# Storing the gate/up operands of later passes in pairs, with their order made to fit and one sum moved between passes

## The chip, the cores and the metric

The kernel runs on one core of a Trainium2 chip. The metric is the time of one execution in microseconds (us), measured on the device; less is better. Each engine has its own instruction stream: TensorE (PE in the profile, PEld for its weight loads), VectorE (DVE), ScalarE (ACT), GpSimd (POOL) and SyncE (SP), which here issues transfers. The granted clock is TensorE's clock as a share of its full speed, the DMA share the mean busy share of the 16 DMA engines, SBUF the memory on the chip that the engines work in.

## The reference

```python
def reference(x, w_gate, w_up, w_down):      # x: 8 x 1024 x 1024, float32; hidden 1024, intermediate 4096
    gate = x @ w_gate
    up = x @ w_up
    gate = 0.5 * gate * (1 + np.tanh(np.sqrt(2 / np.pi) * (gate + 0.044715 * gate ** 3)))
    h = gate * up
    return (h @ w_down).astype(np.float32)
```

## The kernel before

The kernel works on 1024 tokens at a time, in 8 passes. Each pass has a gate/up stage and a down stage. The block products are not the plain ones: passes 0 to 2 use a scheme with 7 products for each 2 x 2 block ("pairs" of block columns, 16 a pass), later passes a finer one whose left operands are 24 signed sums of weight blocks for each of 8 column groups. Those 24 operands are not made when they are needed. They are made once, 12 in pass 1 and 12 in pass 2, in the idle time of VectorE (sums) and ScalarE (plain signed copies), and stored in a DRAM tensor `wop`, from which passes 3 to 7 load two at a time, in rows of 4 KB.

```python
A_PARTS = ([8, 11, 12, 13, 16, 18, 22, 24, 25], [9, 10, 14, 15, 17, 19, 20, 21, 23])
wop = nc.dram_tensor("w_ops", (NQ, NCH, P, 2, 1024), FP16, kind="Internal").ap()
...
    def make_entry(p, q, e):
        n, sign = A_ENTRIES[e]
        v = place[q, n] = places[turn[0] % len(places)]      # 12 slots in SBUF, used in turn
        turn[0] += 1
        if n < 8:                                            # a raw block: a copy on ScalarE
            nc.scalar.activation(four(v), a_node(p, q, n), COPY, scale=float(sign))
        else:                                                # a sum of two nodes: VectorE
            _, op, a, b = A_SUMS[n - 8]
            combine(four(v), op, a_node(p, q, a), a_node(p, q, b))
        nc.sync.dma_start(out=wop[q, e // 2, :, e % 2], in_=v)   # half of each 4 KB row
...
    # gate_up_one, inside the loop over the 16 pairs i = 2 q + e of passes 1 and 2:
            for j, n in enumerate(entries_of(p - FAST + 2)):
                if j // 6 == e:
                    at(2 * (j % 6) + 2, make_entry, p, q, n)     # after products 2, 4, ... 12 of the pair
```

A pair is 14 products of 4 matmuls each. The products are summed in PSUM banks, the buffers that TensorE writes; the next product that takes a bank must wait until VectorE or ScalarE has read what it needs there (an eviction). The order of products and what follows each of them matters below (w is 0 for gate and 1 for up; cut and set closer than in the kernel):

```python
SEQ = [
    ("P1", 0), ("P1", 1), ("P5", 0), ("P6", 0), ("P6", 1), ("P5", 1), ("P7", 0),
    ("P7", 1), ("P2", 0), ("P4", 0), ("P4", 1), ("P2", 1), ("P3", 0), ("P3", 1),
]
AFTER1 = {   # after product k: evictions by ScalarE (copy, snap, gelu), sums by VectorE (add, h)
    1: ["copy 0"], 2: ["copy 1"], 4: ["snap s2 0"], 5: ["snap s2 1"], 7: ["snap s3 0"],
    8: ["snap s3 1", "add s3 0"], 9: ["gelu11", "gelu s3", "add s3 1"],
    10: ["gelu21", "prod s3"], 11: ["h21"], 12: ["h11"], 13: ["add s2 0"], 14: ["add s2 1"],
}
CHAIN = {"P1": "a", "P6": "a", "P7": "a", "P4": "a", "P5": "b", "P3": "b", "P2": "c"}   # PSUM bank
```

## Time and profile before

| | before |
|---|---|
| time, median of 3 runs | 2256.19 us (2256.08 to 2257.9) |
| profiled span, granted clock | 2254.4 us, 1.0 |
| TensorE busy | 2246.1 us |
| gate/up of pass 1 and of pass 2, each | 193.39 us |
| DMA share there | 0.91 and 1.00 |
| stores of operands | 192 of 256 KB, in rows of 2 KB |

The profile is read from the engine that sets the end. Its waits tell what holds it up, and the chain of waits shows which stretch of time belongs to whom. A busy share of another engine, and the DMA share too, says nothing of the end as long as TensorE waits for none of it. The prediction shows the lines.

### The profile page before, as it was taken

The page shows a single profiled execution, that of the slowest core. Times are in us where ns is not written, and L with a number is a line of the kernel's source. Part 1 is how long each engine was busy: PE and PEld are TensorE (multiplying, and loading weights), DVE is VectorE, ACT ScalarE, POOL GpSimd, SP SyncE. Part 2 cuts the span into 40 slices and gives each one's busy share as a digit, 9 for nine tenths or more (in the row PEclk, how much of TensorE's full clock was granted, in tenths as well). Part 3 has the DMA queues.
Part 4 walks back from the last instruction along what each step waited for, and adds up shares of the span by engine and source line. Part 5 has one row for each costly group of instructions (what it writes and reads, how often), then busy time and mean ns, then how long its engine had stood idle before and what let it go on. Part 6 is the DMA issues. An engine that isn't in the chain of part 4 may idle for free.

```text
span 2254.4 us, 42805 instructions
## 1 busy us (share of the span) xinstructions
PE 2246.1 (100%) x16634; PEld 1625.6 (72%) x16634; DVE 1561.7 (69%) x2190; ACT 956.1 (42%) x1866; POOL 679.3 (30%) x825
## 2 busy tenths in 40 slices
PE   9999999999999999999999999999999999999999
PEld 4444444444444445888888888888888888888888
DVE  6576458883588755777776677666786667866674
ACT  4444135651355622666125550356404653055520
POOL 1332013330133200555014550255403543044520
PEclk9999999999999999999999999999999999999999
DMA  9898969989999999999998999989999889988876
GB/s 241 163 207 218 284 184 241 263 264 283 255 227 249 282 309 349 328 342 370 302 339 274 317 304 318 322 270 324 311 324 316 285 308 326 311 311 277 289 285 225
DMA packets 308093, 642.46 MB, mean 285 GB/s; under 512 B 79088, under 2 KB 185328, under 8 KB 287344
## 3 DMA queue, kind: packets, MB, share of 16 engines
q1 hardware_dynamic: 253104, 566.57, 73.2%
q0 software_dynamic: 54784, 73.14, 19.3%
q8 instruction: 130, 2.13, 0.4%
q14 instruction: 75, 0.61, 0.1%
HBM read 574.36 MB, written 138.41 MB: 316 GB/s over the span
## 4 chain that ended last, share of the span: by engine, by line
PE 87%; DMA 2%; SPq 0%; DVE 0%; issue 0%; DVEq 0%
PE ps L848 40%; PE ps L1099 20%; PE ps L626 17%; PE ps L991 10%; DMA wd_quads<-x_sums 1%; SPq L255 0%; DMA ring<-wd_ops 0%; DVE x_sums L452 0%; DVE h_a L923 0%; DVE tmp L1168 0%; DVE x_sums L278 0%; SPq L487 0%; DVEq L278 0%; SPq L535 0%
## 5 line engine op out<-in xcount | busy, mean ns | idle before, releaser
L848 PEld LDWEIGHTS <-ring 128*128 128x128 f16 x8320 | 814.1, 98 | 94.4
L825 POOL TENSOR_TENSOR h_a<-tmp 128x256 f16<-128x256 f32 x640 | 469.3, 753 | 839.3 <-ACT tmp L813 831.9
L848 PE MATMUL ps<-x_sums,ring 128*128 128x256 f16 x5760 | 655.8, 273 | 0.0
L810 DVE TENSOR_TENSOR tmp<-tmp,ps 128x512 f32<-128x512 f32 x640 | 414.5, 683 | 148.1 <-PE ps L848 99.7
L626 PEld LDWEIGHTS <-ring 128*128 128x128 f16 x2632 | 257.5, 98 | 310.4
L795 ACT COPY tmp<-ps 128x512 f32<-128x512 f32 x520 | 304.1, 585 | 237.5 <-PE ps L848 162.8
L626 PE MATMUL ps<-x_sums,ring 128*128 128x512 f16 x1504 | 339.8, 379 | 0.0
L813 ACT ACTIVATE tmp<-tmp 128x256 f32<-128x256 f32 x640 | 264.1, 418 | 172.8 <-DVE tmp L808 79.4
L848 PE MATMUL ps<-x_b,ring 128*128 128x256 f16 x2560 | 305.6, 273 | 0.0
L808 DVE TENSOR_TENSOR tmp<-ps,tmp 128x512 f32<-128x512 f32 x240 | 165.4, 689 | 145.2 <-ACT tmp L795 101.0
L626 PE MATMUL ps<-x_b,ring 128*128 128x512 f16 x1128 | 259.1, 379 | 0.0
L652 POOL TENSOR_TENSOR h_a<-tmp 128x512 f16<-128x512 f32 x94 | 144.5, 1537 | 374.8 <-ACT tmp L650 271.9
L1099 PEld LDWEIGHTS <-h_a 128*128 128x128 f16 x2240 | 219.2, 98 | 25.4
L991 PE MATMUL ps<-ring,h_a 128*128 128x512 f16 x1024 | 222.3, 379 | 0.4 <-DMA ring<-wd_ops 0.4
L1099 PE MATMUL ps<-ring,h_a 128*128 128x256 f16 x1920 | 216.1, 273 | 0.0
L991 PEld LDWEIGHTS <-h_a 128*128 128x128 f16 x1152 | 112.7, 98 | 136.6 <-DMA ring<-wd_ops 0.9
L645 DVE TENSOR_TENSOR tmp<-ps,tmp 128x512 f32<-128x512 f32 x188 | 127.2, 683 | 112.6 <-ACT tmp L637 111.1
L1156 ACT ACTIVATE tmp<-ps 128x512 f32<-128x512 f32 x60 | 35.3, 597 | 362.6 <-PE ps L1099 274.6
L1168 DVE SCALAR_TENSOR_TENSOR tmp<-ps,tmp 128x512 f32<-128x512 f32 x120 | 81.1, 690 | 97.5 <-PE ps L1099 66.6
L351 DVE TENSOR_TENSOR ring<-ring 128x1024 f16<-128x1024 f16 x188 | 138.7, 751 | 11.1 <-DMA ring<-in_w_up_dram 6.9
L637 ACT COPY tmp<-ps 128x512 f32<-128x512 f32 x188 | 109.9, 586 | 77.8 <-PE ps L626 77.8
L1099 PE MATMUL ps<-ring,x_sums 128*128 128x256 f16 x1120 | 126.3, 273 | 0.0
(102 smaller groups left out, 1532.0 us busy)
## 6 DMA issues: line engine op xcount, KB each, us to landing
ring<-w_ops SPq DMA_DIRECT2D x480, 512.0 KB, 5.0
ring<-wd_quads SPq DMA_DIRECT2D x110, 1024.0 KB, 7.0
ring<-wd_ops SPq DMA_DIRECT2D x35, 1024.0 KB, 8.2
out_dram<-tmp SPq DMA_DIRECT2D x128, 256.0 KB, 6.6
w_ops<-h_s SPq DMA_DIRECT2D x128, 256.0 KB, 6.7
ring<-in_w_gate_dram POOLq DMA_DIRECT2D x23, 1024.0 KB, 10.5
ring<-in_w_up_dram POOLq DMA_DIRECT2D x23, 1024.0 KB, 17.8
wd_quads<-x_sums SPq DMA_DIRECT2D x131, 128.0 KB, 6.4
```

What stands on the lines that cost most here:

```text
L351: nc.vector.tensor_tensor(o, a, b, op)
L626: nc.tensor.matmul(ps(b, w), lhs[:, k], rhs[:, k, :], start=(first and k == 0), stop=(k == KH - 1), skip_group_check=True,)
L645: nc.vector.tensor_tensor(o, ps("b", w), o, ADD)
L652: nc.gpsimd.tensor_tensor(hq[TO[n]][:, i, :], tmp[:, t[n, 1]], tmp[:, t[n, 0]], MUL)
L795: nc.scalar.copy(tmp[:, t[o[1]]], ps_all[:, bank[o[2]]])
L808: nc.vector.tensor_tensor(d, b, a, SUB)
L810: nc.vector.tensor_tensor(d, a, b, ADD if o[4] == "add" else SUB)
L813: nc.scalar.activation(d, d, GELU, scale=GSC)
L825: nc.gpsimd.tensor_tensor(h, tmp[:, t[o[1]], MQ : 2 * MQ], g, MUL)
L848: nc.tensor.matmul(ps_all[:, bank[c], w * MQ : (w + 1) * MQ], lhs[:, w, k], rhs[:, k], start=(first and w == 0 and k == 0), stop=(k == KH ...
L991: nc.tensor.matmul(ps_all[:, bank[b, g]], lhs[:, j, g * P : (g + 1) * P], dc[:, n, :], start=(first and j == 0), stop=(j == NP - 1), skip_ ...
L1099: nc.tensor.matmul(ps_all[:, bank[c], m * MQ : (m + 1) * MQ], lhs[:, j, m * P : (m + 1) * P], rhs[:, j, :], start=(first and j == 0 and m ...
```

## The change

The intent is to make transfers cheaper in the two stages that make operands. Two operands that share a 4 KB row are made one after the other, lie side by side in SBUF and are stored by one transfer. To get such neighbours the order of the 24 operands is written out by hand, and sum 21 goes from pass 2 to pass 1 while a plain copy goes the other way (in full: copies 2 and 3 go to pass 2 and copy 7 comes to pass 1). Below, "the order" means the written-out order with this exchange, as opposed to the wider stores.

```diff
--- before.py
+++ after.py
@@ -60,7 +60,10 @@
     (23, 22, 4, False),
 ]
 
-A_PARTS = ([8, 11, 12, 13, 16, 18, 22, 24, 25], [9, 10, 14, 15, 17, 19, 20, 21, 23])
+A_PARTS = (
+    [16, 8, 11, 12, 22, 21, 25, 24, 13, 4, 18, 7],
+    [9, 3, 10, 23, 2, 15, 17, 20, 14, 6, 19, 1],
+)
 
 AFTER = {
     1: [('snap', 's8', 1)],
@@ -356,6 +359,7 @@
         xc[:, j * 1024 : (j + 1) * 1024] for j in range(8, 12)
     ]
     turn = [0]
+    made_last = [None]
 
     def four(v):
         return v.rearrange("p (w k n) -> p w k n", w=2, k=KH)
@@ -375,18 +379,20 @@
         else:
             _, op, a, b = A_SUMS[n - 8]
             combine(four(v), op, a_node(p, q, a), a_node(p, q, b))
-        nc.sync.dma_start(out=wop[q, e // 2, :, e % 2], in_=v)
+
+        if turn[0] % 2 == 0 and e % 2 and made_last[0] == (q, e - 1):
+            k = (turn[0] - 2) % len(places)
+            v = hf["s3"][:, k * 1024 : (k + 2) * 1024] if k < 8 else xc[:, k * 1024 : (k + 2) * 1024]
+            nc.sync.dma_start(
+                out=wop[q, e // 2], in_=v.rearrange("p (e n) -> p e n", e=2)
+            )
+        elif (e ^ 1) not in entries_of(0 if p < FAST - 1 else 1):
+            nc.sync.dma_start(out=wop[q, e // 2, :, e % 2], in_=v)
+        made_last[0] = (q, e)
 
     def entries_of(part):
-        sums = [n for n, _, _, _ in A_SUMS if n in A_PARTS[part]]
-        plain = [n for n, _ in A_ENTRIES if n < 8][3 * part : 3 * part + 3]
-        nodes = []
-        for j, n in enumerate(sums):
-            nodes.append(n)
-            if j % 3 == 1:
-                nodes.append(plain[j // 3])
         ids = [n for n, _ in A_ENTRIES]
-        return [ids.index(n) for n in nodes]
+        return [ids.index(n) for n in A_PARTS[part]]
 
 
 
```

Two operands of each pass still have their partner in the other pass (11 and 23, 12 and 10); those are stored alone.

## The prediction

> **What bounds the kernel now.** I read first the busy times of the page, then the waits of TensorE alone, then the chain that ended last in order of time, then busy time by stage and by pair of column blocks, and last the queue's waits.
>
> The page's first part, a total for each engine:
>
> ```profile
> span 2254.4 us, 42805 instructions
> PE 2246.1 (100%) x16634; PEld 1625.6 (72%) x16634; DVE 1561.7 (69%) x2190; ACT 956.1 (42%) x1866; POOL 679.3 (30%) x825
> ```
>
> TensorE is busy for all but 2254.4 - 2246.1 = 8.3 us. A busy matmul row can hide a slow one, so the total is not yet proof. The waits of TensorE alone (engine and line, what it waited for: us in total, times, longest) name everything it ever waited for:
>
> ```profile
> PE ps L1219 <- DVE h_s L1222: 1.6, 1, 1.6
> PE ps L1198 <- DVE x_b L305: 1.1, 2, 0.6
> PE ps L1198 <- ACT ring L331: 0.6, 1, 0.6
> PE ps L991 <- DMA ring<-wd_ops: 0.4, 1, 0.4
> PE ps L303 <- DVE h_a L297: 0.2, 1, 0.2
> ```
>
> All are of pass 0: its warm-up and first pair, and one load in its down projection. None is on a line that pass 1 or 2 reaches with a wait. The chain in order of time (start us, us, what) shows the rest as one unbroken TensorE stretch from 279.69 to 2250.10 us:
>
> ```profile
> 279.69 27.80 PE ps L991 x128
> 307.50 193.39 PE ps L626 x896
> 500.88 96.69 PE ps L991 x448
> 597.57 193.39 PE ps L626 x896
> 790.96 96.69 PE ps L991 x448
> 887.65 181.68 PE ps L848 x1664
> ```
>
> The two rows of 193.39 us are gate/up of passes 1 and 2, the only stages that the change edits. They have the same length to 10 ns, and 193.39 / 896 = 0.2158 us for a 512-column matmul; the stage after takes 181.68 / 1664 = 0.1092 us for one of 256 columns. That is a steady rate, not a rate with holes in it.
>
> **What the Trainium skill says.** "TensorE: Matmul & The Clock Gate", section "Back-to-back issue gap", gives N / 2.4 + 2.5 ns at full clock: 215.8 ns for 512 columns and 109.2 for 256. The trace agrees to a tenth of a nanosecond, so these stages are at the matmul rate itself. (The same section's other figure, 131 ns sustained at N=512, is not seen here.) "Perfetto Trace Analysis", section "DMA Optimizations", says that going from 2 KB to 4 KB transfers is the primary remedy "when HBM utilization is high but DMA-bound". The first half holds in passes 1 and 2 (DMA share 0.91 and 1.00 in the table below), the second doesn't: TensorE waits for no transfer there. "SBUF — State Buffer", section "Who interferes with whom", says that a VectorE instruction with two SBUF inputs contends with a GpSimd one that reads SBUF. The trace fits that: the same half-width sum takes 0.41 us at its usual and 1.74 us at 407.90 us, beside a GpSimd product. So one more sum on VectorE may cost more than its usual 0.68 us.
>
> **The change part by part.** Busy time by stage (stretch, length, then PE, PEld, DVE, ACT, POOL busy with counts, granted clock, DMA share, GB/s), gate/up of pass 1 and of pass 2:
>
> ```profile
> 307.50:500.88 193.38, 193.38 (x897) 87.66 (x896) 155.87 (x241) 115.46 (x190) 62.79 (x44) 1.00 0.91 237
> 597.57:790.96 193.39, 193.39 (x898) 87.65 (x896) 154.67 (x241) 115.25 (x190) 61.74 (x46) 1.00 1.00 256
> ```
>
> *Stores.* Each of 8 column groups makes 24 operands, 12 in each pass. Before, each is stored alone: 8 x 24 = 192 transfers of 256 KB in rows of 2 KB. After, five of the six double slots a pass hold both members of a storage pair, made one after the other; two operands a group have their partner in the other pass (23 and 11, 10 and 12). So 8 x 2 x (5 + 2) = 112 transfers; a comparison of the two builds confirms 1249 rows of the transfer queue against 1169, and the same instructions in the same order on TensorE. Bytes are unchanged. In the trace's packets the median 2 KB packet of these stages takes 84 to 86 ns and the 4 KB packet of later stages 159 ns, so two for one saves some 11 ns. 80 transfers x 128 rows x 11 ns / 16 engines = 7 us of DMA time out of about 370, plus 80 x 0.32 us = 26 us of issuing on a queue that mostly sleeps. On the path: 0, for nothing waits for these stores before pass 3, where the first comes due long after.
>
> *One sum moved.* Node 21 goes from pass 2 to pass 1, a plain signed copy the other way. 8 sums x some 0.75 us (0.68 alone, 0.88 to 0.95 in the groups that meet GpSimd) = 6 us: VectorE in pass 1 from 155.9 to about 162, in pass 2 from 154.7 to about 149. 8 copies x 1.054 us = 8.4 us: ScalarE from 115.5 to about 107 and from 115.3 to about 124. Both stay far below 193.4. On the path: 0 as long as the order within a pair holds, which is the real question.
>
> *The order within a pair.* A pair of blocks takes 193.39 / 16 = 12.09 us of TensorE. Two neighbouring pairs of pass 1:
>
> ```profile
> 404.20:416.28 12.08, 12.08 (x57) 5.49 (x56) 12.08 (x20) 7.18 (x12) 4.44 (x4) 1.00 0.92 180
> 416.28:428.37 12.09, 12.09 (x57) 5.49 (x56) 8.95 (x17) 7.94 (x13) 4.60 (x3) 1.00 1.12 316
> ```
>
> VectorE is full in the even pair and lags; in the odd one it idles 3.1 us and catches up. In pass 1 the even pair now carries six sums in place of five. In pass 2 it carries four in place of five, so pass 2 gets easier here. What can bite TensorE is the first bank that a late VectorE gives back: product h21 of one pair releases the bank that the third product of the next pair takes. I set each h21's end against that product's start (pair start plus two products of 0.863 us). The margin in pass 1's even pairs is 1.4 us at the least (the pair at 404.20) and 1.9 to 3.4 in the others. A sum of 0.68 us ahead of it leaves 0.7 at the least, so still no wait.
>
> ScalarE in pass 2 has a similar spot: a 1.05 us copy now falls after the fourth product of even pairs, between two evictions of 0.585 us. The second eviction has 1.10 us in hand today. It then ends at about 4.08 + 1.05 + 0.59 = 5.7 us of the pair against a bank needed at 7 x 0.863 = 6.04: some 0.35 us left. The sum over all parts is 0.0 us.
>
> **The rivals.**
> *A new wait of TensorE on VectorE or ScalarE.* For it: margins of 0.7 and 0.35 us are small, and a sum that meets GpSimd can take a microsecond longer. Against it: only one pair of pass 1 comes near, and pass 2's copy has no other copy in front of it. If four pairs lost 0.3 us each, it would make 1.2 us: about 2257.4. If all 16 even pairs lost half a microsecond, 8 us: 2264, still the same verdict.
> *Transfers as the hidden bound, so that wider rows pay.* For it: a DMA share of 0.9 to 1.0, and the queue's own waits (126.8 us on VectorE in front of these stores, shown below). Against it: those waits end with the sum that the store needs, not with a transfer, and TensorE's list has no transfer after 280 us. The whole of what it could give is the 0.4 us there, in a stage that isn't changed: 2255.8.
>
> ```profile
> SPq L378 <- DVE h_s L278: 126.8, 73, 3.9
> SPq L378 <- DMA w_ops<-h_s: 5.6, 8, 1.1
> ```
>
> *A late slot.* A pair's first operand waits for its second before its store starts, so its slot comes free later, by about 1.7 us. There are 12 slots and 12 operands in two pairs of blocks (24.2 us), and stores land in 3.5 to 7 us; worth 0.
>
> **Range and chances.** Nothing is removed from TensorE's 2246.1 us and nothing that it waited for is touched, so the time stays at the median of before, 2256.2 us. Downward only run-to-run spread counts (2256.08 to 2257.9 before) and at most 0.4 us; upward the same spread and a few small new waits. I take 2255.2 to 2258.6. Two per cent is 45 us. Faster by that would need work taken off TensorE, which doesn't happen; slower would need 2.8 us lost in each of the 16 even pairs, more than the largest delay I can construct. Chances 0.005 faster, 0.985 the same, 0.01 slower.
>
> **What would show it.** Right: the chain again has two TensorE rows of 193.39 us; the list of TensorE's waits has the same five rows; 80 stores of 512 KB and 32 of 256 KB; VectorE and ScalarE near 162 and 107 us in pass 1, 149 and 124 in pass 2; a slightly lower DMA share there. Wrong: a new row in TensorE's waits for an eviction or a sum, most likely in the even pairs of pass 1, with rows over 193.39 us; or a shorter row, which would mean that the matmul rate itself depends on the stores and my reading of the bound is false.

## The result, and the profile after

The changed kernel took 2256.88 us (median of 6 runs, 2254.42 to 2257.2), the kernel before 2256.44 us in 6 runs beside it (2256.08 to 2257.9). The ratio is 0.9999 with a 95% interval of 0.9986 to 1.0012: the same. A ratio here is the mean time of one kernel's fast runs over that of the other's of the same rounds, so it is not quite the ratio of the medians quoted.

The changed file has six more lines, so line numbers in its profile are larger: L632 is before's L626 (matmuls of gate/up), L997 is L991 (down), L651 is L645 (the adds), L281 is L278 (the sums), L378 is L374 (the plain copies). The page's totals, and the waits of TensorE alone:

```profile
span 2255.0 us, 42663 instructions
PE 2245.1 (100%) x16634; PEld 1625.1 (72%) x16634; DVE 1558.5 (69%) x2190; ACT 954.9 (42%) x1866; POOL 676.3 (30%) x825
```

```profile
PE ps L1225 <- DVE h_s L1228: 1.6, 1, 1.6
PE ps L306 <- DVE h_a L300: 1.5, 2, 1.3
PE ps L997 <- DMA ring<-wd_ops: 1.2, 1, 1.2
PE ps L1204 <- DVE x_b L308: 1.1, 2, 0.6
PE ps L1204 <- ACT ring L334: 0.6, 1, 0.6
```

They are the same five, all in pass 0. Two of them have other sizes (1.5 for 0.2 us, 1.2 for 0.4); in the experiments below, whose pass 0 has the same instructions up to that point, the transfer's wait is anything from 0 to 2.5 us and that for h_a from 0.3 to 1.8 us in total, so this is spread. The chain that ended last, in order of time:

```profile
308.55 193.39 PE ps L632 x896
501.94 96.69 PE ps L997 x448
598.63 193.39 PE ps L632 x896
```

The two rows that the change could touch have 193.39 us, to the digit what they had. Busy time by stage (pass 1, pass 2; columns as in the prediction):

```profile
308.55:501.94 193.39, 193.39 (x897) 87.67 (x896) 158.90 (x248) 108.15 (x183) 64.66 (x44) 1.00 0.90 236
598.63:792.01 193.38, 193.38 (x897) 87.69 (x896) 148.21 (x233) 122.16 (x199) 58.04 (x46) 1.00 1.00 255
```

Everything moved except the time. VectorE went from 155.87 to 158.90 us in pass 1 and from 154.67 to 148.21 in pass 2; ScalarE from 115.46 to 108.15 and from 115.25 to 122.16. The DMA share hardly moved. The stores themselves did get cheaper, as the queues' lines in pass 1 show (packets, MB, share of 16 engines; q1 carries what SyncE issues, q0 what GpSimd issues, mostly the casting loads, which turn float32 weights into float16), first before, then after:

```profile
q1 hardware_dynamic: 18421, 32.75, 48.0%
q0 software_dynamic: 12762, 12.85, 42.3%
```

```profile
q1 hardware_dynamic: 12729, 32.67, 45.9%
q0 software_dynamic: 12768, 12.86, 44.0%
```

The same bytes in nearly a third fewer packets took 2.1 points of 193.4 us less, 4.1 us; the loads on the other queue, with the same bytes and packets, took 1.7 points more, 3.3 us.

### The profile page after: what moved, and what is told of

It reads as the page before. It is cut to its first block, busy times and chain, and to the rows that moved or that the text cites. A ratio compares the mean times of both kernels' runs of the same rounds, so it can differ in the third digit from the quotient of the medians.

```text
span 2255.0 us, 42663 instructions
## 1 busy us (share of the span) xinstructions
PE 2245.1 (100%) x16634; PEld 1625.1 (72%) x16634; DVE 1558.5 (69%) x2190; ACT 954.9 (42%) x1866; POOL 676.3 (30%) x825
## 4 chain that ended last, share of the span: by engine, by line
PE 99%; DMA 1%; DVE 0%; SPq 0%; ACT 0%; issue 0%; DVEq 0%
PE ps L854 40%; PE ps L632 25%; PE ps L1105 20%; PE ps L997 13%; PE ps L1204 1%; DMA ring<-wd_ops 0%; DMA x_sums<-in_w_gate_dram 0%; DVE x_b L308 0%; SPq L297 0%; ACT ring L334 0%; PE ps L306 0%; DVE tmp L1174 0%; DVEq L308 0%
## 5 line engine op out<-in xcount | busy, mean ns | idle before, releaser
L632 PEld LDWEIGHTS <-ring 128*128 128x128 f16 x2632 | 257.6, 98 | 310.3
L632 PE MATMUL ps<-x_sums,ring 128*128 128x512 f16 x1504 | 339.8, 379 | 0.0
L632 PE MATMUL ps<-x_b,ring 128*128 128x512 f16 x1128 | 259.1, 379 | 0.0
L997 PE MATMUL ps<-ring,h_a 128*128 128x512 f16 x1024 | 222.3, 379 | 1.2 <-DMA ring<-wd_ops 1.2
L997 PEld LDWEIGHTS <-h_a 128*128 128x128 f16 x1152 | 112.6, 98 | 137.4 <-DMA ring<-wd_ops 1.7
L651 DVE TENSOR_TENSOR tmp<-ps,tmp 128x512 f32<-128x512 f32 x188 | 127.8, 686 | 114.4 <-ACT tmp L643 112.6
```

The lines of the kernel that those rows point to most:

```text
L632: nc.tensor.matmul(ps(b, w), lhs[:, k], rhs[:, k, :], start=(first and k == 0), stop=(k == KH - 1), skip_group_check=True,)
L651: nc.vector.tensor_tensor(o, ps("b", w), o, ADD)
L997: nc.tensor.matmul(ps_all[:, bank[b, g]], lhs[:, j, g * P : (g + 1) * P], dc[:, n, :], start=(first and j == 0), stop=(j == NP - 1), skip_ ...
```

## The experiments

Twelve kernels ran. Where a gate/up row is quoted for a kernel whose chain breaks it into pieces, it is the time from its first matmul to the first of the next stage, read from the matmuls' starts in the trace. Margins below are read from the matmuls' starts too. The rows of the chain begin 0.16 to 0.17 us later than the first matmul of the stage (307.50 for 307.33 us), because they begin where the modelled end of the matmul before lies; the prediction and the expectations took pairs' starts from the chain, so their margins are that much too wide.

### 1. The order without the wider stores

```diff
-        if turn[0] % 2 == 0 and e % 2 and made_last[0] == (q, e - 1):
-            ...one transfer for both...
-        elif (e ^ 1) not in entries_of(0 if p < FAST - 1 else 1):
-            nc.sync.dma_start(out=wop[q, e // 2, :, e % 2], in_=v)
+        nc.sync.dma_start(out=wop[q, e // 2, :, e % 2], in_=v)
```

> The changed kernel with its new order of operands, but each operand stored alone in rows of 2 KB (192 stores of 256 KB). My theory (TensorE sets the end; neither part of the change is on its path): two gate/up rows of 193.39 us in the chain, the same five waits of TensorE, ratio to the kernel before 1.000 within 0.001; ScalarE busy about 108 us in pass 1 and 122 in pass 2 as in the changed kernel, since that comes from the order alone. Rival (the two parts have effects that cancel): this one is off by over 2 us in the chain rows, and the stores give it back.

Measured: correct, 2255.92 us (2255.45 to 2256.72, 4 runs) against 2256.25 for the kernel before, ratio 0.9997 (0.998 to 1.0013), both rows 193.39 us, the same waits of TensorE. ScalarE was busy 108.13 and 122.11 us, VectorE 158.92 and 148.46. All as expected: the two parts do not cancel; neither reaches the end. The queues had 47.9% and 42.3% in pass 1, as before the change. The fall on one queue and the rise on the other therefore come with the wider stores, not with the order (one profiled execution of each kernel).

### 2 to 4. Do the transfers have room? Stores made worse

The kernel before, with four transfers of 512 B rows for each operand:

```diff
-        nc.sync.dma_start(out=wop[q, e // 2, :, e % 2], in_=v)
+        for s in range(4):
+            c = slice(256 * s, 256 * (s + 1))
+            nc.sync.dma_start(out=wop[q, e // 2, :, e % 2, c], in_=v[:, c])
```

> The kernel before, with each of the 192 operands stored by four transfers in rows of 512 B: 768 stores of 64 KB, the opposite of what the change does, and four times as strong. Theory: the DMA share and the stores' landing time go up, but TensorE waits for none of it, 193.39 us rows and about 2256 us again. Rival (transfers are a hidden bound at a share of 0.9 to 1.0): TensorE gets waits for ring tiles or weights in passes 1 and 2 and the time goes up by 10 us or more.

Measured: 2398.64 us (one run), 142 us more. My expectation failed: I had taken "TensorE waits for no transfer" for "transfers have a lot of room". Rows: 237.99 and 249.68 us; the down stages behind them took 116.99 and 118.03 us in place of 96.69.

Two runs tell the number of transfers, the width of rows and the bytes apart. Four transfers of 32 partitions each keep rows of 2 KB:

```diff
+        for s in range(4):
+            r = slice(32 * s, 32 * (s + 1))
+            nc.sync.dma_start(out=wop[q, e // 2, r, e % 2], in_=v[r])
```

> The kernel before with each operand stored by four transfers of 32 partitions, rows of 2 KB as before: 768 transfers of 64 KB, as many as in the run with rows of 512 B, which took 2398.64 us. Theory A (the number of transfers on the one queue costs): about 2400 us again. Theory B (the narrow rows cost): near 2256 us.

Measured: 2354.04 us (one run), 98 us more. So most of the 142 us comes with the number of transfers at unchanged row width, and some 45 us with the narrower rows; neither theory was right alone. A transfer of 32 partitions may also use fewer of the 16 engines, which these runs do not separate. The DMA share of pass 1 is lower than before in both, 0.83 here and 0.78 with the narrow rows, and SyncE waits for its own earlier stores before it issues the next (39.1 us in total here, 89.5 with the narrow rows). The engines are less full than before; I read this as the queue's stream being late, which no run shows by itself. (The granted clock was 0.98 over both runs. In pass 1 it was 0.97 here and 0.94 with the narrow rows, with stretches in which the matmuls start 427 ns apart in place of 216; behind pass 2 and its down stage, where TensorE has no gaps, it was 1.00 again. It is part of the time lost.)

A second copy of every operand into a tensor that nobody reads doubles stores and bytes and leaves the row width:

```diff
         nc.sync.dma_start(out=wop[q, e // 2, :, e % 2], in_=v)
+        nc.sync.dma_start(out=wop2[q, e // 2, :, e % 2], in_=v)
```

> The kernel before with every operand stored a second time into a tensor that nobody reads: 384 stores in rows of 2 KB, 50 MB more. DMA shares of 0.91 and 1.00 in passes 1 and 2 leave little for 8 percent more bytes of the kernel in those 387 us. Theory (transfers are next in line but have some room because loads run two column groups ahead): the casting loads of the weights come late, TensorE waits, 30 to 100 us more. Rival (the share of 1.0 overstates how full the engines are): within 5 us of before.

Measured: 2335.14 us (one run), 79 us more, inside the 30 to 100 expected, with TensorE waiting for casting loads (7.6 us), for down operands (12.0 us) and for VectorE and ScalarE. Its line for gate/up of pass 1:

```profile
308.53:526.26 217.73, 200.25 (x898) 88.03 (x896) 157.92 (x241) 115.20 (x190) 64.49 (x44) 0.98 1.06 303
```

It moved 303 GB/s at a share of 1.06, where the kernel before moved 237 at 0.91. A share of one is thus not a ceiling of bytes. But the room that is left is small: twice the stores is too much. The stores are off the path at their present cost, and close to it.

### 5 and 6. How late may VectorE be in pass 1?

```diff
             _, op, a, b = A_SUMS[n - 8]
-            combine(four(v), op, a_node(p, q, a), a_node(p, q, b))
+            again = 2 if p == FAST - 2 and n == 11 else 0        # and 4
+            for _ in range(1 + again):
+                combine(four(v), op, a_node(p, q, a), a_node(p, q, b))
```

> The changed kernel with the third sum of each even pair of pass 1 made three times in place of once (two more VectorE sums, same result), ahead of the product that gives back the bank. In the changed kernel the least margin there is 1.56 us; sums follow each other every 0.60 us, so 1.2 us are eaten and some 0.35 us are left in the tightest pair. Theory: no wait of TensorE or one or two of under 0.5 us in pass 1, row 193.4 to 194.4 us. Rival (VectorE has no influence at all on TensorE): exactly 193.39 here, and also with four more sums.

> The same with four more sums in each even pair of pass 1: 2.4 us against margins of 1.56 to 2.57 us. Theory: TensorE waits for VectorE in the four or five even pairs whose margin is 1.56 to 1.90 us, 0.5 to 0.9 us each, so the gate/up row of pass 1 gets 2 to 5 us longer, and pass 2 stays at 193.39. Rival (no influence): 193.39 in both.

Measured: 2260.45 us and 2270.25 us (one run each); pass 1's row went to 197.74 and 207.93 us, pass 2 stayed at 193.39. That VectorE reaches TensorE when it is late enough is shown. The sizes are wrong: I expected at most 1 and then 2 to 5 us, and got 4.35 and 14.5. The waits of TensorE with two more sums name where:

```profile
PE ps L634 <- DVE tmp L653: 0.9, 5, 0.2
...
PE ps L634 <- DVE h_a L671: 0.5, 1, 0.5
```

The list is not complete. The matmuls' starts show 15 breaks in the row, 4.40 us in all: eight at products 13 and 14 of four even pairs (2.41 us, behind an add) and seven at product 3 of odd pairs (1.99 us, behind product h21, whose bank I had watched). With four more sums there are 14 of the first kind (12.26 us) and 7 of the second (2.34 us). Products 13 and 14 are P3, which goes into the bank that "add s3" reads after products 8 and 9. That is a second deadline on VectorE, and it is the tighter one. For the pair that the prediction shows at 404.20 us before, the second add of s3 is this line of the timeline (start, us, engine, line):

```profile
414.10 0.68 DVE L645 TENSOR_TENSOR tmp<-ps,tmp 128x512 f32<-128x512 f32 x1
```

It ends at 414.78, and product 14 starts at 415.25 (the pair's first matmul at 404.02, and 13 x 0.863 us): 0.47 us in hand, where h21 has 1.25. In the changed kernel the same pair's first matmul starts at 405.08:

```profile
414.68 0.68 DVE L651 TENSOR_TENSOR tmp<-ps,tmp 128x512 f32<-128x512 f32 x1
```

It ends at 415.36 against 416.30, 0.94 us in hand; the least of all pairs is 0.80. Four of the seven full even pairs have 0.80 to 0.95 us there and three have 1.6. Two more sums take 1.2 us, which is past it in the four, and four take 2.4, which is past it in all seven: so the breaks lie.

At h21 the changed kernel has 1.40 to 2.40 us in hand in these pairs, so 1.2 us would not have been too much. But in each of the seven one more sum then ran beside a GpSimd product and took 1.75 us (1.49 in one) in place of 0.68, such as this one with two more sums:

```profile
343.38 1.76 DVE L281 TENSOR_TENSOR h_s<-h_s 128x1024 f16<-128x1024 f16 x1
```

In that pair h21 came some 2.5 us later than in the changed kernel, against 2.40 in hand. The prediction had named this, a sum that meets GpSimd and takes a microsecond longer; the expectation had left it out.

The third error is what a listed wait stands for. The waits listed for gate/up with two more sums add to 1.4 us, the row grew by 4.35. One break with an idle time of 13 ns puts the next matmul 176 ns late, one of 204 ns 367 ns late: 0.163 us more than the idle time, at every break. This is not a cost of the break but the way idle time is counted: it begins at the modelled end of the matmul before, 379 ns after its start, where in an unbroken stream the next matmul starts after 216 ns. A break of 96 ns in pass 0 of a later run (after_copy_half) has no idle time at all. Besides, the list left out the nine breaks of this row with 123 ns of idle time or less.

### 7 and 8. How late may ScalarE be in pass 2?

```diff
             nc.scalar.activation(four(v), a_node(p, q, n), COPY, scale=float(sign))
+            if p == FAST - 1 and n == 3:                  # half: four(v)[:, 0]; in full in the second run
+                nc.scalar.activation(four(v)[:, 0], a_node(p, q, n)[:, 0], COPY, scale=float(sign))
```

> The changed kernel with one more half-width signed copy on ScalarE (0.63 us) behind the full one after the fourth product of each even pair of pass 2. The eviction behind it has 0.48 us of margin in the changed kernel. Theory: TensorE waits 0.1 to 0.2 us for ScalarE in each of 8 pairs, the gate/up row of pass 2 is 0.5 to 1.5 us longer, pass 1 stays at 193.39. Rival (ScalarE has more room, as bank hand-over isn't what the margin measures): 193.39.

> The changed kernel with that copy made twice in full (1.05 us more). Theory: 1.0 - 0.48 = about 0.55 us of wait in each of 8 even pairs of pass 2, so its row is 4 to 5 us longer, pass 1 unchanged. Rival: 193.39.

Measured: 2259.91 and 2262.3 us (one run each); pass 2's row 196.45 and 199.87 us, so 3.06 and 6.48 more where 0.5 to 1.5 and 4 to 5 were expected, pass 1 at 193.39. The wait is there in exactly eight pairs, with half a copy:

```profile
PE ps L636 <- ACT tmp L647: 1.8, 8, 0.2
```

Eight waits of some 0.23 us, yet 3.06 us: 0.38 each. With a full copy the list shows 5.2 us in 8 waits, and the row 6.48: 0.81 each for 0.65. Again the list is 0.16 us short at each break. By the matmuls' starts the eviction behind the plain copy has 0.32 us in hand in the changed kernel (0.37 in the first pair), not 0.48; 0.63 and 1.05 us more then leave 0.31 and 0.73 us of delay, near the 0.38 and 0.81 measured. The margin is real, and the place of the deadline was right here.

### 9 to 11. The same change where TensorE is not the bound

All products of gate/up in passes 1 and 2 lose one of four matmuls. The result is wrong.

```diff
-            for k in range(KH):
+            nk = KH - 1 if 0 < p < FAST else KH
+            for k in range(nk):
```

> A wrong result on purpose: the kernel before with three in place of four accumulating matmuls in every product of gate/up in passes 1 and 2 (448 matmuls fewer). If TensorE alone set the end, 448 x 0.2158 = 96.7 us would go. Theory: TensorE's work in each of these stages is then 145.0 us, less than VectorE's 155.9 and 154.7, so VectorE becomes the bound, the two rows take some 158 to 165 us each, and 57 to 70 us go. Rival (transfers are close behind, share 0.91 and 1.00): the rows stop at 180 us or more, and waits for loads of weights appear.

> A wrong result on purpose: the changed kernel with the same 448 matmuls fewer. Theory: where VectorE is the bound, what the change moved can be seen: pass 1 a little longer (VectorE 158 us against 155.9) and pass 2 shorter (147 against 154.7), in sum 2 to 8 us faster than the shortened kernel before. Rival (transfers are the bound there): faster by 10 us or more in both passes, since the stores became fewer. Second rival: no difference, as the lag within a pair and not the sum counts.

> A wrong result on purpose: the new order with single stores, with the same 448 matmuls fewer. The shortened pair differed by 20.7 us (2233.71 against 2212.99). Theory A (wider rows relieve the transfers, which are next in line): this one stays near the shortened kernel before, 2228 to 2236 us. Theory B (the order within a pair and the moved sum relieve VectorE and ScalarE): near the shortened changed kernel, 2210 to 2218. In between: both.

| 448 matmuls fewer | median of 4 runs, us | ratio to the whole kernel before | pass 1, us | pass 2, us |
|---|---|---|---|---|
| kernel before | 2233.71 | 0.9894 (0.9878 to 0.9911) | 185.88 | 175.47 |
| order alone | 2214.52 | 0.9812 (0.9796 to 0.9829) | 174.42 | 168.73 |
| changed kernel | 2212.99 | 0.981 (0.9795 to 0.9825) | 173.75 | 169.50 |

The arithmetic of busy times failed here: with TensorE's work at 145.0 us, VectorE's 155.9 did not set the row, which took 185.88. TensorE waited in turn for VectorE (33.7 us over both passes, by its list), ScalarE (17.0) and a few loads (2.9). The rival's figure, 180 us or more, was met in pass 1, and the loads do take part, as the waits below show. (The granted clock was 0.96 to 0.98 in pass 1 of all three, so the rows hold some of that too.) And the change, which is worth nothing in the whole kernel, is worth 20.7 us in this one, where 2 to 8 were expected. Nearly all of that, 19.2 us, comes from the order alone; the wider stores add 1.5 us, which the intervals do not resolve. The result lies where Theory B put it, and Theory A is out. The two rows account for 18.1 us of the gain. They are those of the profiled executions, of which that of the kernel before is the slowest of its four (2239.46 us): another 3 to 4 us of the difference there lie in pass 0, which the change does not touch. In the two rows together the wider stores gave nothing (343.15 us for order alone, 343.25 with them); the down stage behind pass 2 took 101.35 and 101.28 us with single stores and 96.69 with pairs, in one execution each.

One place where the order works in pass 1 can be read from GpSimd's waits. Its stream issues the casting loads of weights, each of which must wait for the last reader of the tile it overwrites. In the shortened kernel before, then in the shortened order alone:

```profile
POOL ring L336 <- DVE tmp L646: 26.9, 6, 5.2
```

```profile
POOL ring L339 <- ACT x_sums L378: 3.2, 10, 0.3
```

Six loads, one for each column group of pass 1 that has one, stood 26.9 us behind VectorE, up to 5.2 us each. The old order of pass 1 ends a group with sum 25, of which one operand is raw, so the load waits until a late VectorE has read it (the line names the add that directly follows this sum). The new one ends with copy 7 on ScalarE; its last sum with a raw operand, 18, comes one step earlier. VectorE in turn, which adds up the weights that these loads bring, waited 11.1 us for them in pass 1 of the shortened kernel before and 1.0 us with the new order. The whole kernels show the same, 15.3 us in 5 waits before and none in the changed kernel; the load simply goes out earlier, and nobody there waits for it. In pass 2 both old and new order end their raw reads with copies, so this does not explain the 6 to 7 us there. What the traces show there is that VectorE's sums meet GpSimd less often: 15 instructions of pass 2 took over 0.5 us more than is usual for their shape in the shortened kernel before, 8 in both others, every one of them beside a GpSimd instruction; what all instructions took over the usual fell from 18.5 to 9.6 and 9.4 us (in pass 1 from 17.5 to 13.6 in both). Pass 2 also has 8 sums fewer. TensorE's waits for ScalarE evictions fell from 17.0 to 3.9 us over both passes, which fits. How much each of these is worth was not tried.

### 12. A version for the last wait

The one wait of TensorE for a transfer is in pass 0's down stage: a load stands behind four transposing loads in SyncE's stream. They can be issued one step later.

```diff
-                        if v == (3 - p if p < FAST - 1 else 0):
+                        if v == (4 if p == 0 else 3 - p if p < FAST - 1 else 0):
                             transpose_x(p + 1)
```

> The changed kernel with the four transposing loads of pass 0's down projection issued one step later, so that the load of a down operand no longer stands behind them in the queue. Theory: the one wait of TensorE for a transfer (0.4 us before, 1.2 us after) goes, as the load is issued some 10 us earlier; the time falls by 0.4 to 1.2 us, which is inside the spread of the runs and can be told from the list of waits alone. Rival: the transposed tiles come too late for pass 1 and a new wait of TensorE appears at its start.

Measured: correct, 2255.44 us (2254.98 to 2255.66, 5 runs) against 2256.04, ratio 0.9996 (0.9983 to 1.001). The wait is gone from TensorE's list, which has four rows left and no transfer among them; the down row of pass 0 is 96.69 us like all others, where the changed kernel had 98.11 and the kernel before 97.29. No new wait appears at pass 1. The load is issued at 261.44 us in place of 272.26. But the same wait is also missing in one run without this edit (after_copy_twice, down row 96.69 us), so one trace does not show that the edit removed it, and the gain of up to 1.4 us is not resolved by the times. It is the version I would keep.

## Why the prediction was right or wrong

- **The bound: right.** TensorE alone sets the end from pass 0's down stage on. The rows of 193.39 us, the rate and the five waits were all as told. Experiments 5 to 8 lengthened only the stage that they touched, and through TensorE's breaks there. That the list of waits "names everything" is too strong, as experiment 5 shows; what carries the claim is that the matmuls' starts have no break in either row.
- **Stores: right in number, right in size, wrong in the share.** 112 stores (80 of 512 KB, 32 of 256 KB), and 4.1 us less packet time on that queue in each of the two passes, 8.2 in all for an estimate of 7. "A slightly lower DMA share" is the step that failed: it was 0.90 and 1.00 for 0.91 and 1.00, where 7 us in both passes would have taken off some 0.02, as the casting loads' packets grew by 3.3 us in pass 1 and 2.9 in pass 2 (52.0 to 53.5%). That this comes with the wider stores is shown by experiment 1. Why was not tried. If both queues use the same engines, a packet's time may contain a wait for the other's longer packet; that is only argued. The prediction also took this share for high HBM utilization; it is busy time, not bytes, and experiment 4 moved 303 GB/s where 237 went at 0.91.
- **The moved sum: right direction, sizes off.** Expected VectorE 162 and 149 us, measured 158.90 and 148.21. The term was mis-sized in pass 1, where 8 sums added 3.0 us, not 6: in a row of instructions a sum adds 0.60 us, not 0.75, so 4.8 us, and fewer sums met GpSimd. In the sum of both passes VectorE was busy 3.4 us less with the same number of sums, and experiment 1 has nearly that loss (3.2 us) with single stores too, so it belongs to the order. The traces show where: 24 instructions of the two passes took over 0.5 us more than is usual for their shape before and 18 after, each of them beside a GpSimd instruction, and what all instructions took over the usual fell from 27.7 to 22.7 us, 1.6 of these 5.0 us in pass 1. No run changed this alone. ScalarE, expected 107 and 124, had 108.15 and 122.16.
- **The order within a pair: the right question, with the wrong deadline.** "The first bank that a late VectorE gives back: product h21" is the step that failed. The adds of s3 come due earlier, before products 13 and 14. The least margin was 0.47 us before, not 1.4. In six of the seven full even pairs of pass 1 it fell by 0.3 to 0.9 us with the sum added ahead, as I had it for the other deadline; in the tightest pair it grew by 0.47, so the least is 0.80 after. By the prediction's own sum, 0.68 us ahead of 0.47, a break was due in that pair; that none came is luck as far as this step goes. The trace tells what made up for the sum there: VectorE entered the pair 0.24 us earlier, the last sum of the group before no longer ran at its start (0.60), and the instruction beside a GpSimd product was stretched by 0.25 us less. No run tested it. ScalarE's margin was told as 0.35 and is 0.32.
- **The rival of a new wait: right that it would not come, wrong in its price.** I priced a wait by its idle time. Experiments 5 to 8 show that the delay is 0.16 us more than the listed idle time at each break, and that short ones are not listed.
- **The rival of transfers as the hidden bound: right for this change, too weak in general.** Transfers bind nothing at the present rate, but twice the stores cost 79 us. The share of 0.9 to 1.0 was a warning about what comes next, not about now.
- **The range: right.** 2256.88 lies in 2255.2 to 2258.6; the difference of 0.4 us to the kernel before is within the spread of either.

## What to carry to other kernels

When the trace shows one engine at its own rate without a break, a change beside it is worth nothing, however good it is; where its value went can be seen by shortening that engine's work and running both versions again (here 20.7 us, nearly all with the order and its exchanged sum). Before calling a margin safe, list every deadline of the late engine, also the write that must wait for a read, and price a break by how late the next matmul starts and not by the idle time listed. A full share of another resource does not say that it binds, but make it a little worse before saying that it has room.

## What the Trainium skill lacked or had wrong

- "TensorE: Matmul & The Clock Gate", section "Back-to-back issue gap": the isolated figure holds in a stream of weight loads and matmuls too (215.8 ns for 512 columns), and the sustained one, 131 ns, is not seen.
- "Perfetto Trace Analysis", section "DMA Optimizations", expects that batching from 2 KB to 4 KB "can dramatically improve throughput": here it gave 159 ns a packet for two of 84 to 86, 6 percent, and while the stores' queue lost 4.1 us in a pass, the casting loads' queue gained 3.3. Even in the shortened kernels, where transfers are on the chain, it was worth 1.5 us, inside the interval.
- "Perfetto Trace Analysis" warns that the occupancy of the DMA engines misleads, but no page read has figures for how that share relates to what more can be moved: 237 GB/s at 0.91 and 303 GB/s at 1.06 in the same stage, and with 768 small transfers on one queue 98 us were lost at a share of 0.83.
